# A two-layer decoder trunk on one core: where p's second layer is split, in which order the attention's end is written, and who copies the keys

## The chip, the core and the metric

The kernel runs on one core of one Trainium2 chip. A core has TensorE (PE in the profile, with PEld for its weight loads), VectorE (DVE), ScalarE (ACT), GpSimd (POOL) and SyncE (SP), each with an instruction queue of its own that runs in order, and DMA engines that move data between HBM and SBUF, the 128-partition working memory. TensorE writes its sums to PSUM, from which VectorE and ScalarE read them. The metric is the device time of one execution in microseconds; the kernel before took 1311.96 us (median of three runs, 1311.76 to 1312.21).

## The reference, cut to what matters

Batch 1, 512 tokens, 1024 features, two layers. Layer 0 mixes tokens with a causal convolution module, layer 1 with differential attention of 8 heads, each with two query/key parts of 64 features and values of 128. After each mixer stand a SwiGLU feed-forward network (hidden size 2816) and a gated embedding `p` (two layers of 512 x 256).

```python
def diff_attention(x, w_qkv, q_g, k_g, ..., sub_g, w_o, rel_bias, lambda_init):
    q, k, v = jnp.split(x @ w_qkv, 3, axis=-1)
    q = rms_norm(q.reshape(B, S, N_HEADS, 2, HEAD_DIM), q_g) * (HEAD_DIM ** -0.5)
    k = rms_norm(k.reshape(B, S, N_HEADS, 2, HEAD_DIM), k_g)
    ...
        logits = jnp.einsum('bhcqd,bhckd->bhcqk', q_blk, k) + bias[None, :, None]
        probs = jax.nn.softmax(jnp.where(dist >= 0, logits, -jnp.inf), axis=-1)
        w = probs[:, :, 0] - lam * probs[:, :, 1]
        return jnp.einsum('bhqk,bhkd->bhqd', w, v)
    ...
    o = rms_norm(o, sub_g) * (1.0 - lambda_init)
    return o.reshape(B, S, N_HEADS * V_DIM) @ w_o

for i in range(DEPTH):
    u = rms_norm(h, mixer_norm_g)
    h = h + mixer(u)                                   # conv (i = 0) or attention (i = 1)
    h = h + swiglu(rms_norm(h, ffn_norm_g[i]), w_gate, w_up, w_down)
    gate = sigmoid(rms_norm(h, ple_norm_g[i]) @ ple_w_gate[i])
    h = h + gate * (p[i] @ ple_w_proj[i])
```

All tensors are float32. The kernel keeps that accuracy with float32r matmuls by splitting each operand into a high part (a cast) and a low part (the rest): one product is three matmuls.

## The kernel before

**Split operands.** `weight()` loads 512 KB into one of two raw buffers (`wraw`, SP's queue, L146), casts it on ScalarE into one of four high buffers (`whi`, L149) and subtracts on VectorE, or on GpSimd where it is told to, into one of four low buffers (`wlo`, L150). `mm3()` (L155 to L157) is the three matmuls of one product. Weights are read in the order in which `_layout()` packs them, so the order of the calls of `weight()` is the order of the loads. `pfeatures()` (L249 to L255) loads the two halves of p through the same raw buffers (L252), casts (L253) and subtracts (L254) into the buffers that it is given.

**Buffers.** Every tile has a tag with a number of buffers, and a new tile of that tag waits until an old one has been read for the last time. PSUM has eight banks: four `mm` (sums), two `sc` (scores), two `tp` (transposes). In the attention, tags A0 to A15 hold the split input u and, from the end of the projections on, the split head outputs `ot`; B0 to B7 hold the split values (B0 to B3: heads 0 to 3, a tile for each block of 128 tokens; B4 to B7: heads 4 to 7); C0 to C5 hold two pairs of heads' split queries and keys, two buffers each; D0 to D5 hold unscaled head outputs, one each, head 6 after head 0 and head 7 after head 1.

**Projections.** `QKV` (L80) lists six slabs: queries and keys of the four pairs of heads ("q", 0 to 3) and values of two groups of four heads ("v", 0 and 1), in the order q0, v0, q1, q2, v1, q3. A slab has four weights and four blocks of 128 tokens, each block 24 matmuls of 512 columns (`tokens()`). For a query block, `unit()` scales and squares it on ScalarE, sums per head on VectorE, takes the power on GpSimd (L214), multiplies on GpSimd (L721); `unit_end()`, called inside the next block, transposes it on TensorE (L727) and splits it. A key of 64 features is stored in the half of the partitions that belongs to its part c ("own"); the score product needs its high part in the other half too, since the low part of the query lies there. In the kernel before that copy is a GpSimd instruction (L740), after ScalarE's cast of the own half (L736).

**Attention.** 32 steps, one for each head and block of queries. Each has three stages: `stage_s` (scores L772 and L773, minimum and shift on VectorE L775, exponential on ScalarE L779, the combination of the two softmaxes L782 to L784), `stage_t` two steps later (transposes L792, split L794 and L795) and `stage_a` three steps later (sum over values L808 and L809; after a head's last block the head's norm, L820 to L830). `stage_o` (L834) transposes a finished head and splits it. The stages stand in one list; 63 of its 96 are called between the projections' matmuls (`take`), as many as the paces in `QKV` say.

**The attention's end.** After the projections (L871 to L908) the rest of the list is called by `step()`, one stage a call, which also calls `stage_o` for heads that are due. `pfeatures(1, ...)` comes first, into C0 and C1; then eight times `project()` (the product of p with its weight, two `mm3`, copied out by ScalarE at L271), with a step before and two within; then `linear()`, the output product: the first two chunks of 128 features together, with a step after each `mm3`, the other six one by one, each with a weight of its own. Each chunk is added to h (L905), and the norm of the next layer begins on it.

**Who orders the work.** The program is written with a tile framework that puts each engine's instructions into a fixed order before the run, from a modelled timeline: written order gives the rank, and where the model sees an instruction not ready, a later one of the same engine may go ahead of it. At run time each engine follows that order and waits at semaphores.

Of the kernel before, what the change touches and what calls it, by code (L numbers as in the profile page):

```python
# [69 lines left out]
        TAPS += [(_c, j) for j in range(0, PE_TAPS[_c], 4)]  # L70


KDUP = "G"
HALVES = slice(0, DH), slice(DH, P)
LT = 2
LA = 3
# [8 lines left out]
def trunk(ctx, tc, xT, pT, wts, diag, dww, vec, rel, onehot, lamv, out):  # L85
# [9 lines left out]
    def sb(shape, tag, bufs, dt=F32):  # L95
        uid[0] += 1
        return pool.tile(shape, dt, tag=tag, name=f"{tag}_{uid[0]}", bufs=bufs)
# [40 lines left out]
    def weight(n=1024, pieces=1, between=(), eng=V):  # L138
        i = wnext[0]
        wnext[0] += 1  # L140
        raw = sb([P, 1024], "wraw", 2)
        hi = sb([P, 1024], "whi", 4, F32R)
        lo = sb([P, 1024], "wlo", 4, F32R)
        for k in range(pieces):
            cut = slice(k * n // pieces, (k + 1) * n // pieces)
            loaded[0] = nc.sync.dma_start(raw[:, cut], wts[i, :, cut])  # L146
            if k < len(between):
                between[k]()
            A.copy(hi[:, cut], raw[:, cut])  # L149
            eng.tensor_tensor(lo[:, cut], raw[:, cut], f(hi[:, cut]), ALU.subtract)  # L150
        return hi, lo
# [7 lines left out]
    def wpart(w, k):  # L159
        return tuple(t[:, k * P : (k + 1) * P] for t in w)  # L160

    def both(t):
        return t[:, 0], t[:, 1]
# [85 lines left out]
    def pfeatures(layer, parts):  # L249
        for k, (hi, lo) in enumerate(parts):  # L250
            raw = sb([P, 1024], "wraw", 2)[:, :S]
            nc.sync.dma_start(raw, pT[layer, :, k * S : (k + 1) * S])  # L252
            A.copy(hi, raw)  # L253
            (G if layer == 0 else V).tensor_tensor(lo, raw, f(hi), ALU.subtract)  # L254
        return parts  # L255
# [3 lines left out]
    def project(ph, m, w, o, step=lambda: None):  # L259

        acc = mm()
        for k in range(2):
            mm3(
                acc,
                wpart(w, 2 * (m % 4) + k),
                ph[k],
                k == 0,
                k == 1,
            )
            step()  # L270
        A.copy(o, acc)  # L271
        return o
# [261 lines left out]
            if c >= 2:  # L534
                V.tensor_tensor(z[c - 2][1], y[c - 2], f(z[c - 2][0]), ALU.subtract)

    def linear(n_in, src, consume, group0=1, before=None, after=None, first=0):


        m = 0  # L540
        while m < NC:
            g = group0 if m == 0 else 1
            ws = [weight(n_in * P, eng=G if m == 0 and i >= g - first else V) for i in range(g)]
            accs = [mm() for _ in range(g)]
            for k in range(n_in):
                if before:
                    before(k)
                for w_, a_ in zip(ws, accs):
                    mm3(a_, wpart(w_, k), src[k], k == 0, k == n_in - 1)
                    if after:  # L550
                        after()
            for i in range(g):
                consume(m + i, accs[i])
            m += g
# [112 lines left out]
    def slab(n=0):  # L667
        ws = [weight(eng=G if i < n else V) for i in range(4)]
        return [
            tuple(t[:, j * S : (j + 1) * S] for t in ws[k])  # L670
            for k in range(4)
            for j in range(2)
        ]
# [50 lines left out]
    def unit_end(pair, tb, q):  # L724
        t = tp()
        for i in range(4):
            T.transpose(t[:, i * P : (i + 1) * P], q[:, i * P : (i + 1) * P], ident)  # L727
        t4 = t.rearrange("p (h c t) -> p h c t", h=2, c=2)
        cut = slice(tb * P, (tb + 1) * P)
        qs, ks, kl = qk[pair][0:2], qk[pair][2:4], qk[pair][4:6]  # L730

        qg, kg = gains[:, 0:1], col("k_g")
        for c in range(2):
            own, other = HALVES[c], HALVES[1 - c]
            A.activation(qs[c][own, :, cut], t4[own, :, 0], AF.Copy, scale=qg[own])
            A.activation(ks[c][own, :, cut], t4[own, :, 1], AF.Copy, scale=kg[own])  # L736
            if KDUP == "A":
                A.activation(ks[c][other, :, cut], t4[own, :, 1], AF.Copy, scale=kg[own])
            else:
                G.tensor_copy(ks[c][other, :, cut], f(ks[c][own, :, cut]))  # L740
        for c in range(2):
            own, other = HALVES[c], HALVES[1 - c]
            V.scalar_tensor_tensor(
                qs[c][other, :, cut], t4[own, :, 0], qg[own], f(qs[c][own, :, cut]), ALU.mult, ALU.subtract)
            V.scalar_tensor_tensor(
                kl[c][own, :, cut], t4[own, :, 1], kg[own], f(ks[c][own, :, cut]), ALU.mult, ALU.subtract)
# [87 lines left out]
    def stage_o(hd):  # L834
        t = tp()
        for i in range(4):
            T.transpose(t[:, i * P : (i + 1) * P], osb[hd][:, i * P : (i + 1) * P], ident)  # L837
        hi = sb([P, S], f"A{2 * hd}", 1, F32R)
        lo = sb([P, S], f"A{2 * hd + 1}", 1, F32R)
        split_scaled(t, gains[:, 1:2], hi, lo)  # L840
        ot[hd] = (hi, lo)
# [4 lines left out]
    for n in range(len(todo) + LA):  # L846
        for stage, at in ((stage_s, n), (stage_t, n - LT), (stage_a, n - LA)):
            if 0 <= at < len(todo):
                stages.append((n, partial(stage, *todo[at])))

    def take(n):
        got, stages[:n] = [s for _, s in stages[:n]], []
        return got

    waiting = None
    for what, at, pace in QKV:
        ws = slab(GLO if at > 0 else 0)
        for tb in range(4):
            between = take(3 * pace[tb])
            between += [None] * (6 - len(between))  # L860
            if waiting:
                between.append(partial(unit_end, *waiting))
                waiting = None
            if what == "v":
                values(at, ws, tb, between)
            else:
                waiting = unit(at, ws, tb, between)
    unit_end(*waiting)


    done = [0]  # L871

    def step():
        if stages:
            n, s = stages.pop(0)
            s()
        else:
            n = 99
        while done[0] < NH and (n - LA - 3) // 4 > done[0]:
            stage_o(done[0])  # L880
            done[0] += 1

    ph = pfeatures(1, [both(sb([P, 2, S], t, 2, F32R)) for t in ("C0", "C1")])
    pp = []
    for m in range(NC):
        if m % 4 == 0:
            w = weight()
        step()
        if m < 2:
            o = sb([P, S], f"D{m + 2}", 1)  # L890
        elif m % 2 == 0:
            o2 = sb([P, 2, S], f"C{m // 2 + 1}", 2)
            o = o2[:, 0]
        else:
            o = o2[:, 1]
        pp.append(project(ph, m, w, o, step))

    def heads_until(k):
        while done[0] <= k:
            step()  # L900

    norm = Norm("ffn_g1")

    def add_attn(m, acc):
        V.tensor_tensor(h[m], acc, h[m], ALU.add)  # L905
        norm.chunk(m)

    linear(NC, ot, add_attn, 2, heads_until, step)  # L908
    n2 = Norm("ple_g1")
    ffn(norm, n2)  # L910

# [131 lines left out]
```

## Time and profile before

| What | us |
|---|---|
| median of three runs | 1311.96 |
| the profiled execution, its own time | 1313.88 |
| its span | 1312.1 |
| TensorE busy in the span | 1276.4 |
| VectorE | 759.3 |
| ScalarE | 526.9 |
| GpSimd | 276.1 |
| the first query block is scaled (L711) | 650.0 |
| the last projection's last matmul starts | 806.63 |
| first product of p's second layer starts | 819.75 |

A row of the stages' view gives a stretch of the span, its length, each engine's busy time in it with the number of instructions, TensorE's granted clock as a share of full speed, the mean busy share of the DMA engines and GB/s. A row of the waits gives who waited for whom: microseconds in total, number of waits, the longest. A row of the timeline gives start, duration, engine, line, operation, output and input tile, how many instructions are merged into it and, in brackets, how long the engine sat idle before it and what released it. Matmuls are pipelined: one may start before the last one's end, so the distance of their starts, not their duration, is what each costs. A row of the groups gives count, busy time, mean of one in nanoseconds, and idle time before them.

### The profile page before, as it was taken

What the parts mean: (1) busy time and instruction counts of PE and PEld (TensorE: products, weight loads), DVE (VectorE), ACT (ScalarE), POOL (GpSimd) and SP (SyncE); (2) the same over time, 40 slices, a digit from 0 to 9 for tenths busy, and PEclk for the clock granted to TensorE, in tenths of its full rate; (3) what the DMA queues carried; (4) which work ended last, traced back from release to release, by engine and by line L of the source; (5) the groups of instructions that cost most, each with busy time, mean ns of one, the idle gap of its engine ahead of it and who ended that gap; (6) DMA issues with size and microseconds to landing.
All of it is one profiled execution on the core that took longest, in us unless ns stands there. A gap on an engine that the chain in (4) does not pass through costs nothing. (4 is left out here: it accounts for less than half of the span.)

```text
span 1312.1 us, 15285 instructions
## 1 busy us (share of the span) xinstructions
PE 1276.4 (97%) x5830; PEld 1047.4 (80%) x5830; DVE 759.3 (58%) x1168; ACT 526.9 (40%) x832; POOL 276.1 (21%) x219
## 2 busy tenths in 40 slices
PE   8999889999999999999999998999999999999998
PEld 5787668888888888888888886778888888888887
DVE  6998866544344434455678888945543344334445
ACT  5644255332123212253566767734332233223332
POOL 4839533000000000022345534122000000000030
PEclk8999889999999999999999998999999999999999
DMA  5554203332333232232222221213233323222231
GB/s 193 182 179 156 81 32 113 96 97 80 113 96 96 81 112 96 77 116 94 72 97 81 86 75 49 97 33 128 97 96 97 96 97 97 96 96 88 80 122 64
DMA packets 44534, 129.21 MB, mean 98 GB/s; under 512 B 5123, under 2 KB 8835, under 8 KB 44460
## 3 DMA queue, kind: packets, MB, share of 16 engines
q1 hardware_dynamic: 42912, 125.84, 29.2%
q10 hardware_dynamic: 1548, 2.39, 0.6%
q8 instruction: 46, 0.75, 0.2%
q14 instruction: 28, 0.23, 0.1%
HBM read 124.52 MB, written 3.69 MB: 98 GB/s over the span
## 5 line engine op out<-in xcount | busy, mean ns | idle before, releaser
L149 ACT CAST whi<-wraw 128x1024 fp32r<-128x1024 f32 (+2 forms) x214 | 218.5, 1026 | 563.5 <-PE mm L157 363.1
L155 PE MATMUL mm<-A,wlo 128*128 128x512 f32 (+1 forms) x1096 | 425.6, 392 | 9.5 <-ACT A L533 5.9
L156 PE MATMUL mm<-A,whi 128*128 128x512 f32 (+1 forms) x1096 | 428.9, 392 | 0.7 <-DVE A L170 0.5
L157 PE MATMUL mm<-A,whi 128*128 128x512 f32 (+1 forms) x1096 | 426.5, 390 | 0.0
L150 DVE TENSOR_TENSOR wlo<-wraw,whi 128x1024 fp32r<-128x1024 f32 (+2 forms) x207 | 257.5, 1248 | 66.6 <-ACT whi L149 66.2
L155 PEld LDWEIGHTS mm<-A,wlo 128*128 128x128 f32 x1096 | 207.2, 189 | 55.2 <-ACT A L533 6.7
L156 PEld LDWEIGHTS mm<-A,whi 128*128 128x128 f32 x1096 | 207.0, 189 | 48.0 <-DVE A L170 3.8
L157 PEld LDWEIGHTS mm<-A,whi 128*128 128x128 f32 x1096 | 207.0, 189 | 43.3 <-issue 1.3
L189 POOL TENSOR_TENSOR acc<-acc,wk 128x512 f32<-128x512 f32 x42 | 68.6, 1634 | 786.7 <-issue 673.3
L156 PE MATMUL mm<-B,whi 128*128 128x512 f32 x352 | 137.5, 391 | 0.0
L157 PE MATMUL mm<-B,whi 128*128 128x512 f32 x352 | 137.5, 391 | 0.0
L155 PE MATMUL mm<-B,wlo 128*128 128x512 f32 x352 | 137.1, 391 | 0.0
L591 DVE TENSOR_TENSOR h<-mm,h 128x512 f32<-128x512 f32 x48 | 33.0, 691 | 123.1 <-PE mm L157 123.0
L583 DVE TENSOR_TENSOR big<-mm,rb 128x512 f32<-128x512 f32 x44 | 30.4, 691 | 126.2 <-PE mm L157 126.2
L581 DVE TENSOR_TENSOR big<-mm,rb 128x512 f32<-128x512 f32 x44 | 30.4, 691 | 99.0 <-PE mm L157 92.6
L157 PEld LDWEIGHTS mm<-B,whi 128*128 128x128 f32 x352 | 66.1, 188 | 14.5
L156 PEld LDWEIGHTS mm<-B,whi 128*128 128x128 f32 x352 | 66.0, 188 | 14.3
L155 PEld LDWEIGHTS mm<-B,wlo 128*128 128x128 f32 x352 | 66.1, 188 | 14.2
L157 PE MATMUL mm<-whi,A 128*128 128x512 f32 x192 | 75.6, 395 | 0.0
L156 PE MATMUL mm<-wlo,A 128*128 128x512 f32 x192 | 75.0, 396 | 0.0
L155 PE MATMUL mm<-whi,A 128*128 128x512 f32 x192 | 74.8, 396 | 0.0
L214 POOL TENSOR_TENSOR r<-v,mhalf 128x8 f32<-128x8 f32 (+1 forms) x31 | 47.4, 1530 | 114.6 <-DVE v L212 92.4
(207 smaller groups left out, 1439.0 us busy)
## 6 DMA issues: line engine op xcount, KB each, us to landing
wraw<-in_wts SPq DMA_DIRECT2D x194, 512.0 KB, 3.5
wraw<-in_wts SPq DMA_DIRECT2D x16, 384.0 KB, 2.9
D<-in_diag SPq DMA_DIRECT2D x19, 256.0 KB, 4.7
C<-in_diag SPq DMA_DIRECT2D x12, 256.0 KB, 5.5
h<-in_xT SPq DMA_DIRECT2D x8, 256.0 KB, 5.3
bias<-scr ACTq DMA_DIRECT2D x8, 256.0 KB, 3.5
out_t<-h SPq DMA_DIRECT2D x7, 256.0 KB, 2.0
wraw<-in_wts SPq DMA_DIRECT2D x4, 256.0 KB, 4.8
```

Source lines behind the costliest of these rows:

```text
L149: A.copy(hi[:, cut], raw[:, cut])
L150: eng.tensor_tensor(lo[:, cut], raw[:, cut], f(hi[:, cut]), ALU.subtract)
L155: T.matmul(acc, al, bh, start=first, stop=False)
L156: T.matmul(acc, ah, bl, start=False, stop=False)
L157: return T.matmul(acc, ah, bh, start=False, stop=last)
L189: self.eng.tensor_tensor(self.acc, self.acc, sq, ALU.add)
L214: last_pow[0] = G.tensor_tensor(r[:, :n], v[:, :n], mhalf[:, :n], ALU.pow)
L581: V.tensor_tensor(tg, pg, rb, ALU.mult)
L583: V.tensor_tensor(tu, pu, rb, ALU.mult)
L591: V.tensor_tensor(h[m], acc, h[m], ALU.add)
```

## The change

Three things are changed.

1. The second layer's p is split during the last query slab: `pfeatures(1, ...)` is called after that slab's four weights, before its first block of tokens, into tiles of tags B0 and B1 (the values of heads 0 to 3, token blocks 0 and 1). Before it was called after the projections, into C0 and C1.
2. The end is written as a loop over the remaining steps. First p's two weights and the output product's first two are requested. Each turn of the loop calls all stages of one step, then `stage_o` for heads that are due, then one piece of `fill`: two `factor()` (one chunk of p's product), five `first_sums(k)` (head k's part of the first two output chunks, six matmuls), two `factor()`. After the loop come the last head's `stage_o`, the other four `factor()` and `first_sums` of 5 to 7. `linear()` goes on with the third chunk; its hooks for steps are gone.
3. The keys' copy to the other half of the partitions is a transfer issued on ScalarE's queue, in place of a GpSimd instruction: 32 of them, 64 KB each (64 partitions, two rows of 512 bytes).

```diff
-KDUP = "G"
...
-    def linear(n_in, src, consume, group0=1, before=None, after=None, first=0):
+    def linear(n_in, src, consume, group0=1, first=0, start=0):
-        m = 0
+        m = start
         while m < NC:
...
             for k in range(n_in):
-                if before:
-                    before(k)
                 for w_, a_ in zip(ws, accs):
                     mm3(a_, wpart(w_, k), src[k], k == 0, k == n_in - 1)
-                    if after:
-                        after()
...
             A.activation(ks[c][own, :, cut], t4[own, :, 1], AF.Copy, scale=kg[own])
-            if KDUP == "A":
-                A.activation(ks[c][other, :, cut], t4[own, :, 1], AF.Copy, scale=kg[own])
-            else:
-                G.tensor_copy(ks[c][other, :, cut], f(ks[c][own, :, cut]))
+            nc.scalar.dma_start(f(ks[c][other, :, cut]), f(ks[c][own, :, cut]))
...
+    def take_to(n):
+        got = [s for at, s in stages if at < n]
+        del stages[: len(got)]
+        return got
...
         ws = slab(GLO if at > 0 else 0)
+        if at == 3:
+            ph = pfeatures(1, [both(sb([P, 2, S], f"B{k}", 1, F32R)) for k in range(2)])
         for tb in range(4):
...
-    done = [0]
-    def step():
-        if stages:
-            n, s = stages.pop(0)
-            s()
-        else:
-            n = 99
-        while done[0] < NH and (n - LA - 3) // 4 > done[0]:
-            stage_o(done[0])
-            done[0] += 1
-    ph = pfeatures(1, [both(sb([P, 2, S], t, 2, F32R)) for t in ("C0", "C1")])
+    pw = [weight(), weight()]
+    wo = [weight(), weight()]
     pp = []
-    for m in range(NC):
-        if m % 4 == 0:
-            w = weight()
-        step()
+    oaccs = []
+    def factor():
+        m = len(pp)
         if m < 2:
             o = sb([P, S], f"D{m + 2}", 1)
         elif m % 2 == 0:
-            o2 = sb([P, 2, S], f"C{m // 2 + 1}", 2)
-            o = o2[:, 0]
+            o2[0] = sb([P, 2, S], f"C{m // 2 + 1}", 2)
+            o = o2[0][:, 0]
         else:
-            o = o2[:, 1]
-        pp.append(project(ph, m, w, o, step))
-    def heads_until(k):
-        while done[0] <= k:
-            step()
+            o = o2[0][:, 1]
+        pp.append(project(ph, m, pw[m // 4], o))
+    o2 = [None]
+    def first_sums(k):
+        if k == 0:
+            oaccs.extend([mm(), mm()])
+        for w_, a_ in zip(wo, oaccs):
+            mm3(a_, wpart(w_, k), ot[k], k == 0, k == NC - 1)
+    fill = [factor] * 2 + [partial(first_sums, k) for k in range(5)] + [factor] * 2
+    done = 0
+    while stages:
+        n = stages[0][0]
+        for s in take_to(n + 1):
+            s()
+        while done < NH and (n + 1 - LA - 3) // 4 > done:
+            stage_o(done)
+            done += 1
+        if fill and (not hasattr(fill[0], "args") or fill[0].args[0] < done):
+            fill.pop(0)()
+    stage_o(NH - 1)
+    for _ in range(NC - len(pp)):
+        factor()
+    for k in range(5, NH):
+        first_sums(k)
...
-    linear(NC, ot, add_attn, 2, heads_until, step)
+    for m in range(2):
+        add_attn(m, oaccs[m])
+    linear(NC, ot, add_attn, start=2)
```

## The prediction

> **What bounds the kernel now.** I read the head of the page and the forty slices first, then the busy times by stage, the waits of TensorE around the one place where it is not full, and the timeline of that place.
>
> ```profile
> span 1312.1 us, 15285 instructions
> PE 1276.4 (97%) x5830; PEld 1047.4 (80%) x5830; DVE 759.3 (58%) x1168; ACT 526.9 (40%) x832; POOL 276.1 (21%) x219
> PE   8999889999999999999999998999999999999998
> PEclk8999889999999999999999998999999999999999
> ```
>
> TensorE is the bound: 97% busy, and between the start and the last slice its only dip is at slice 25 (32.8 us each, so 787 to 820), where the clock row dips too. That is the attention's end, so the stages there come next.
>
> ```profile
> core 0: us, PE busy (x) PEld busy (x) DVE busy (x) ACT busy (x) POOL busy (x), PEclk, DMA share, GB/s
> 660.00:805.00 145.00, 142.73 (x748) 121.22 (x747) 116.72 (x307) 96.28 (x222) 68.85 (x67) 1.00 0.22 74
> 805.00:820.00 15.00, 8.77 (x45) 7.19 (x44) 14.63 (x37) 12.27 (x29) 5.36 (x7) 0.76 0.27 87
> 820.00:835.00 15.00, 13.06 (x64) 10.15 (x64) 14.11 (x38) 11.99 (x27) 3.95 (x4) 0.89 0.43 141
> 835.00:852.00 17.00, 17.00 (x107) 15.15 (x106) 14.77 (x48) 13.46 (x36) 2.05 (x2) 1.00 0.19 63
> 852.00:872.00 20.00, 19.79 (x105) 16.72 (x104) 7.07 (x20) 4.04 (x8) 4.09 (x4) 1.00 0.01 2
> 872.00:880.00 8.00, 5.47 (x26) 4.03 (x24) 5.84 (x7) 4.89 (x7) 1.88 (x2) 1.00 0.10 31
> ...
> 810.00:815.00 5.00, 2.20 (x10) 1.50 (x10) 4.92 (x14) 4.42 (x13) 2.79 (x3) 0.79 0.35 75
> 815.00:820.00 5.00, 2.59 (x11) 2.52 (x12) 4.91 (x14) 3.10 (x6) 1.27 (x2) 0.50 0.47 187
> 820.00:825.00 5.00, 5.00 (x18) 4.08 (x18) 4.86 (x13) 3.17 (x7) 2.54 (x4) 0.68 0.66 213
> ```
>
> From 660 to 805 TensorE lacks 2.27 of 145 us. From 805 to 880 it lacks 6.23 + 1.94 + 0 + 0.21 + 2.53 = 10.91 us. On top it ran below full clock: 2.20 x (1 - 0.79) + 2.59 x (1 - 0.50) + 5.00 x (1 - 0.68) = 0.46 + 1.30 + 1.60 = 3.36 us of busy time were the clock's. So **14.3 us** are there to win in this stage, of which 9.6 lie in 805 to 825 (idle 15 + 5 - 8.77 - 5.00 = 6.23, and all the 3.36). VectorE is 14.63 of 15 busy there, then 14.11 of 15, then 14.77 of 17: it is the second bound until about 852.
>
> ```profile
> PE sc L772 <- DVE st L775: 4.2, 4, 1.7
> PE sc L772 <- DVE st L783: 2.5, 1, 2.5
> PE mm L155 <- DVE wlo L150: 1.8, 1, 1.8
> PE tp L727 <- DVE C L745: 1.0, 1, 1.0
> PE mm L155 <- ACT A L169: 0.8, 1, 0.8
> PE sc L772 <- POOL C L740: 0.2, 1, 0.2
> ```
>
> TensorE waits for the softmax's VectorE work because it has nothing else queued. Why not, the timeline tells:
>
> ```profile
> 781.33 2.32 SPq L252 DMA_DIRECT2D wraw<-in_pT  x2
> ...
> 794.61 1.04 POOL L830 TENSOR_TENSOR D<-D,r 128x512 f32<-128x512 f32 x1 [0.34 <-ACT acc L779]
> ...
> 806.63 0.40 PE L157 MATMUL mm<-whi,A 128*128 128x512 f32 x1
> ...
> 809.01 1.16 ACT L253 CAST C<-wraw 128x512 fp32r<-128x512 f32 x2
> 812.18 0.68 DVE L254 TENSOR_TENSOR C<-wraw,C 128x512 fp32r<-128x512 f32 x1
> 813.06 0.68 DVE L254 TENSOR_TENSOR C<-wraw,C 128x512 fp32r<-128x512 f32 x1
> 812.89 8.05 SPq L146 DMA_DIRECT2D wraw<-in_wts  x4
> 816.88 1.04 ACT L149 CAST whi<-wraw 128x1024 fp32r<-128x1024 f32 x1 [2.06 <-DMA wraw<-in_wts]
> 818.10 1.22 DVE L150 TENSOR_TENSOR wlo<-wraw,whi 128x1024 fp32r<-128x1024 f32 x1
> 819.75 0.78 PE L155 MATMUL mm<-C,wlo 128*128 128x512 f32 x1
> ...
> 877.99 0.50 PE L155 MATMUL mm<-A,wlo 128*128 128x512 f32 x1 [1.75 <-DVE wlo L150]
> ```
>
> p's two raw parts are issued at 781.33 into the only two raw weight buffers and sit there until they are split at 809.01 to 813.7, because their split form goes to C0 and C1, which the queries and keys of heads 4 and 5 hold. Only at 812.89, as the first part is done (812.18 + 0.68), can the next weight be issued; it is cast at 816.88, its low part made at 818.10, and the first p product runs at 819.75, though the last queries' matmul ended at about 806.9. From 806.9 to 819.75 TensorE has only scores, transposes and sums that wait on each other.
>
> **The change part by part.** The unit first: matmuls of 512 columns one after another.
>
> ```profile
> 878.80 0.40 PE L155 MATMUL mm<-A,wlo 128*128 128x512 f32 x1
> ...
> 893.12 0.39 PE L155 MATMUL mm<-A,wlo 128*128 128x512 f32 x1
> ```
>
> 63 matmuls start from the first to the second, so one takes 14.32 / 63 = 0.227 us. A `factor()` and a `first_sums()` are 6 each, 1.36 us; the eight factors hold 10.9 us.
>
> *p's parts in B0 and B1.* These hold values of heads 0 to 3, free when head 3's sums are out; head 3 is the fourth of eight to be scaled, at 794.61, and its sums end some microseconds before. Two casts (1.16 us on ScalarE) and two subtractions (2 x 0.68 on VectorE) move from 809 to 813.7 to some 790 to 796, inside a stretch where VectorE is 116.72 of 145 and ScalarE 96.28 of 145 busy and TensorE full: costed at nothing, cover the queries' matmuls; without it, 1.16 + 0.68 = 1.8 us. The two raw buffers come free 17 us earlier, so SP's queue moves on: p's two weights can land long before 806 and wait only for the four split buffers of the last queries, which free one by one in the last block of tokens. Best case they are ready at 806.9, when the factors can start; worst, VectorE (4.92 and 4.91 of 5 in two of the slices) pushes the two subtractions behind stage work, some 2 x 1.25 = 2.5 us each way, and the factors start near 812. With 10.9 us of factors against a pocket of 12.9 (806.9 to 819.75) the pocket can be nearly filled. What stays: the waits in which each engine's fixed order misses by a fraction, and the outputs of factors 0 and 1, which need D2 and D3, hence heads 2 and 3 transposed. The bounds are 9.6 (all) and 9.6 x 5 / 12.9 = 3.7 less, 5.9; if ready only after 815 about 3. I take **-7.0**.
>
> The granted clock is part of this: 0.50 in 815 to 820, and 0.68 while TensorE was 5.00 of 5.00 busy, so it returned only after some 3 us of steady work. The Trainium skill (TensorE: Matmul & The Clock Gate, Part 1: The HAM clock gate) has two states, half and full, and a full busy window of about 3.4 us before the full one returns; the trace agrees with its means. By that rule the clock's share is all or nothing: 9.0 or 5.6 for the sum of 8.0 below.
>
> *Written order of the end.* Before, three stages and a factor alternate, then one stage per three output matmuls; after, all stages of one step and then one of two factors, five first sums, two factors, and the last four factors and three first sums behind the last head. VectorE's work until the last scores (852) stays the same but for 1.36 moved away, so this stretch gets no shorter than VectorE allows: 14.11 + 14.77 of 32 us from 820. I cost the 1.94 us idle in 820 to 835 as kept: factors spent earlier are missing there, the first sums stand in. At the end, 0.8 us go to the last head's transposed output and 1.8 to a weight's low part at 877.99 (four buffers held by the four open output chunks). After, four factors and two first sums (36 x 0.227 = 8.2 us) cover the first, and the third and fourth chunk's weights take the buffers that p's weights leave, so the next ones aren't all due at once. Of 2.53 I take **-2.0**; bounds 0 (the stall moves to a later chunk) and -2.5.
>
> *Keys by transfers.* 32 GpSimd copies go; 32 issues on ScalarE's queue come.
>
> ```profile
> L740 POOL CAST C<-C 64x256 fp32r<-64x256 f32 x32 | 14.6, 455 | 21.1 <-ACT C L736 19.9
> L647 ACTq DMA_DIRECT2D bias<-scr x8: 326/326/455, 647.6 to 812.0; - x8
> C<-pi SPq DMA_DIRECT2D x12, 64.0 KB, 3.3
> B<-po SPq DMA_DIRECT2D x12, 64.0 KB, 1.9
> ```
>
> TensorE waited 0.2 us for these copies near the end (above); GpSimd is not the bound, so its 14.6 us are worth nothing but that. A transfer of the same 64 KB landed 1.9 to 3.3 us after issue against 0.46, so the copied half comes 1.5 to 2.8 us later. Its reader is the score stage of that token block, one or more blocks later (24 matmuls, 5.4 us, each); only in the last two blocks is the lag near the cover. Each issue takes 0.33 us, and it must wait for the cast just ahead of it on the same engine; behind it queue the second half's casts, the exponentials and the splits of transposed weights. 32 x 0.33 = 10.4 us on an engine with 48.7 of 145 us free. No ScalarE-issued copy of ScalarE's own result is in the trace, so bounds: -0.2 (the wait above gone) and +10.4 (every issue shown on TensorE). It lies nearer the low end, as nearly all falls where TensorE is full and fed from four accumulators, but eight issues (2.6 us) fall in 804 to 821 where ScalarE is 12.27 of 15: **+1.0**.
>
> Sum: -7.0 - 2.0 + 1.0 = -8.0. The profiled execution took 1313.9 us with a span of 1312.1; the median of the three shown is 1311.96, so the span goes to 1304.1 and the median to about **1304.0**.
>
> **The rivals.** *Everything is filled*: also the waits of 820 to 835 go, and the copies cost nothing: -14.3 plus some 1.3 of unavoidable misses, 1299. For it: there is work enough (10.9 of factors, 6.8 of first sums). Against: VectorE's 43.5 busy us (14.63 + 14.11 + 14.77) must pass before the last head can end.
>
> *VectorE is the bound*: the low parts come at 812 or later and idle time only moves behind 820, where factors are now missing: -3 from the first pocket, 1309. For it: 4.92 and 4.91 of 5; against: VectorE is 14 of 15 there because stages ran ahead while nothing else could.
>
> *ScalarE's queue turns the sign*: each transfer holds ScalarE's queue until the cast before it is written, then 0.33 us; the transposes' buffers come free later, q and k of the next block with them, and score stages slip. With every issue shown: -9 + 10.4, and two more waits of the mean length of those on L775 (4.2 / 4 = 1.05 each), = +3.5, 1315.5. It decides from an exposure of 9 / 32 = 0.28 us for each copy, less than one issue. For it: ScalarE at 82% from 805 to 820; against: 34% free before. The Trainium skill (DMA: Bandwidth & Descriptors, Anatomy of one DMA) says that a wait of a DMA is taken on the issuing sequencer before dispatch, which is this mechanism; no row of before shows such a wait.
>
> *The change doesn't do what it says*: each engine's order is planned from a model, and p's splits may still be planned late, or the raw buffers be held by another load: 1312.
>
> **How the numbers follow.** Forecast 0.46 (about 1301.5 to 1307), all filled 0.14, VectorE 0.17, ScalarE's queue 0.16, not as said 0.07. Range 1298.5 to 1314: the first four reach into it, the upper part of the fourth is left out. I count 0.2% (2.6 us) as what can be told from no change: faster is the first three less a little (0.75), same 0.07, slower 0.18.
>
> **What would show it.** Right: L254 near 790, weights of p cast by 806, the first p product within 2 us of the last queries' matmul, clock 1.00 from 805 to 825, TensorE idle under 4 us from 805 to 880. Wrong: idle of TensorE before L772 between 660 and 805 well over 2.3 us, with ScalarE's casts (L735, L736) spread out around the transfers; or idle on VectorE's results in 820 to 850 that was not there. If the copies' exposure on TensorE is above 0.28 us each, the forecast's sign is wrong.

## The result, and the profile after

| | before | after |
|---|---|---|
| median, us (six runs each, same chip) | 1312.11 (1311.76 to 1313.13) | 1317.47 (1313.67 to 1318.71) |
| ratio, 95% interval | | 1.0037 [1.0024, 1.0050] |

The changed kernel is slower; the forecast was 8 us faster. Executions of one kernel spread here by several microseconds: the profiled one of the changed kernel took 1313.67 (span 1311.9), the other five 1317.2 to 1318.7, so a second profile of it was taken (after_again below, 1317.79, span 1316.0).

Two rows of the forty slices of the changed kernel:

```profile
PE   8999989999999999999999998999999999999998
PEclk8999989999999999999999999899999999999999
```

TensorE's dip in slice 25 is still there, and the clock's, now in slice 26. The busy times by stage, in the columns of before:

```profile
660.00:805.00 145.00, 140.89 (x739) 118.94 (x738) 121.45 (x306) 97.02 (x224) 51.59 (x38) 1.00 0.28 90
805.00:820.00 15.00, 9.44 (x50) 7.54 (x49) 14.69 (x37) 11.95 (x29) 6.71 (x5) 0.88 0.56 175
820.00:835.00 15.00, 14.65 (x72) 12.53 (x73) 11.82 (x35) 8.71 (x21) 2.26 (x2) 0.78 0.04 10
835.00:852.00 17.00, 14.23 (x87) 11.58 (x86) 15.45 (x54) 11.99 (x34) 3.78 (x4) 1.00 0.02 4
852.00:872.00 20.00, 19.82 (x105) 16.72 (x105) 6.50 (x13) 7.27 (x13) 2.79 (x3) 1.00 0.14 50
872.00:880.00 8.00, 6.25 (x28) 4.83 (x27) 5.32 (x6) 4.20 (x6) 2.11 (x2) 1.00 0.14 42
```

From 805 to 880 TensorE lacks 5.56 + 0.35 + 2.77 + 0.18 + 1.75 = 10.61 us, where it lacked 10.91. The clock takes 9.44 x 0.12 + 14.65 x 0.22 = 4.4 us of 805 to 835, where by the same two rows of before it took 8.77 x 0.24 + 13.06 x 0.11 = 3.5. And from 660 to 805 it now lacks 4.11 us in place of 2.27.

A kernel's time is cut most cleanly at three starts on TensorE: the first projection matmul of layer 1, the last one, and the last of the feed-forward network's first 384 matmuls, which follow the output product. (One expectation below calls this last cut the last output matmul. The output product itself ends 88.9 us earlier, at 899.70 before and 899.46 after, and these 88.9 us are the same to 0.03 us in all profiles but keys_glo0's, where they are 89.1. So the end's differences are made ahead of the feed-forward network.) Before (first and last of these; the middle one, 806.63, stands in the prediction), then the change's second profile:

```profile
633.37 0.39 PE L155 MATMUL mm<-whi,A 128*128 128x512 f32 x1
988.56 0.39 PE L157 MATMUL mm<-A,whi 128*128 128x512 f32 x1
```

```profile
632.56 0.39 PE L154 MATMUL mm<-whi,A 128*128 128x512 f32 x1
810.86 0.39 PE L156 MATMUL mm<-whi,A 128*128 128x512 f32 x1
992.46 0.39 PE L156 MATMUL mm<-A,whi 128*128 128x512 f32 x1
```

The *projections* took 806.63 - 633.37 = 173.26 us before and 810.86 - 632.56 = 178.30 after; the *end* 988.56 - 806.63 = 181.93 before and 992.46 - 810.86 = 181.60 after. In the change's first profile they are 175.49 and 182.08. What follows the last cut is 323.5 us in all three. So **the end, from which 9.0 us were expected, gave nothing, and the projections, where 1.0 was to be lost, lost 2.2 to 5.0.** All experiments below are read by these two numbers, taken from each profile in the same way. They leave out the start of layer 1, which wanders by 3 us from one execution to the next (630.4 to 633.5), but not the granted clock: the two profiles of the change differ by 2.8 us in the projections. Each is from one profile only, so the ratio of the whole times stands beside them.

**The projections.** Timelines of GpSimd, VectorE and TensorE in the second profile, and then the busy times by stage, with the clock in the third column from the end:

```profile
742.22 1.04 POOL L822 TENSOR_TENSOR D<-D,r 128x512 f32<-128x512 f32 x1 [1.86 <-DVE st L774]
743.22 2.37 POOL L149 TENSOR_TENSOR wlo<-wraw,whi 128x1024 fp32r<-128x1024 f32 x1
742.21 1.07 DVE L775 SCALAR_TENSOR_TENSOR st<-st,lam 128x1 f32<-128x1 f32 x1
743.31 2.82 DVE L776 SCALAR_TENSOR_TENSOR big<-rb,st,big 128x512 f32<-128x512 f32 x1
746.52 0.33 PE L764 MATMUL sc<-C,C 128*128 128x128 f32 x1 [2.02 <-DVE st L767]
748.08 1.09 PE L722 MATMUL tp<-ident,big 128*128 128x128 f32 x4 [0.72 <-DVE wtl L787]
```

```profile
740.00:745.00 5.00, 4.50 (x25) 3.59 (x23) 4.89 (x9) 4.21 (x7) 3.14 (x3) 1.00 0.23 66
745.00:750.00 5.00, 2.76 (x12) 2.41 (x13) 4.97 (x13) 3.26 (x9) 1.63 (x2) 0.74 0.23 59
750.00:755.00 5.00, 5.00 (x15) 3.89 (x14) 4.55 (x11) 3.62 (x8) 4.28 (x4) 0.58 0.49 180
```

On GpSimd a head's scaling (L822) and a weight's low part (L149) stand back to back, 742.22 to 745.59. Beside them two VectorE steps of the softmax are held: L775 takes 1.07 and L776 2.82 us, each ending right after the GpSimd instruction beside it. Scores on TensorE wait 2.02 us for what comes behind, a transpose 0.72 more. Then the clock reads 0.74 and 0.58. In the first profile the same two waits are there, to the hundredth, but the clock stays at 1.00. In the second it takes 2.76 x 0.26 + 5.00 x 0.42 = 2.8 us in these rows: that is the difference between the two profiles. In before the same low part lies elsewhere:

```profile
740.16 2.39 POOL L150 TENSOR_TENSOR wlo<-wraw,whi 128x1024 fp32r<-128x1024 f32 x1
740.39 2.19 DVE L212 TENSOR_SCALAR v<-v 128x4 f32<-128x4 f32 x1 [0.46 <-POOL r L214]
```

```profile
740.00:745.00 5.00, 5.00 (x28) 4.20 (x27) 4.61 (x5) 2.82 (x6) 5.00 (x4) 1.00 0.25 70
```

It holds up a VectorE instruction too, but a small one that TensorE isn't waiting for (5.00 of 5 busy). The low part stands eight microseconds ahead of the next head's scaling there. What changed is GpSimd's planned order: low part, then scaling before; scaling, then low part after. The Trainium skill (SBUF — State Buffer, SBUF: two separate sides) says that VectorE, with two inputs from SBUF, and a GpSimd instruction that reads SBUF contend for a port pair that one of them holds for its whole instruction while the other stands still. The trace agrees: L776 was through 0.54 us after the end of the GpSimd instruction, and takes 0.75 alone (below).

**The end.** ScalarE's and VectorE's rows for p and its weights, and TensorE's around the products, in the change's first profile:

```profile
787.00 0.69 DVE L253 TENSOR_TENSOR B<-wraw,B 128x512 fp32r<-128x512 f32 x1
788.53 0.68 DVE L253 TENSOR_TENSOR B<-wraw,B 128x512 fp32r<-128x512 f32 x1
805.72 1.04 ACT L148 CAST whi<-wraw 128x1024 fp32r<-128x1024 f32 x1
806.25 0.39 PE L156 MATMUL mm<-whi,A 128*128 128x512 f32 x1
808.43 0.39 PE L154 MATMUL mm<-B,wlo 128*128 128x512 f32 x1
811.07 0.39 PE L156 MATMUL mm<-B,whi 128*128 128x512 f32 x1
819.80 0.66 PE L764 MATMUL sc<-C,C 128*128 128x384 f32 x1 [2.08 <-DVE v L211]
820.58 1.05 PE L829 MATMUL tp<-ident,D 128*128 128x128 f32 x4
826.67 0.57 ACT L270 COPY D<-mm 128x512 f32<-128x512 f32 x1
```

p is split at 787 to 789 and the first product starts at 808.43, 1.8 us behind the end of the queries' last matmul (806.25 + 0.39), as forecast. But only factors 0 and 1 follow, 12 of 48 matmuls, the last at 811.07; ScalarE can copy them out only from 826.67. The list of `fill` goes on with the first sums, which need transposed heads, and the first heads are transposed at 820.58. From 812 to 820 TensorE waits again for the softmax: of 805 to 820 it is idle 5.56 us, where before it was 6.23.

### The profile page after: what moved, and what is told of

Same layout as the page of the kernel before. It is cut to its first block, busy times and chain, and to the rows that moved or that the text cites. A ratio compares the mean times of both kernels' runs of the same rounds, so it can differ in the third digit from the quotient of the medians.

```text
span 1311.9 us, 15291 instructions
## 1 busy us (share of the span) xinstructions
PE 1275.6 (97%) x5830; PEld 1045.4 (80%) x5830; DVE 762.6 (58%) x1168; ACT 527.7 (40%) x832; POOL 262.4 (20%) x187
## 4 chain that ended last, share of the span: by engine, by line
PE 82%; DVE 9%; POOL 3%; issue 2%; ACT 1%; DMA 1%; SPq 0%; ACTq 0%; DVEq 0%; POOLq 0%
PE mm L154 26%; PE mm L155 26%; PE mm L156 26%; DVE sc L401 3%; POOL wk L390 2%; DVE wlo L149 2%; PE mm L800 1%; DVE B L401 1%; PE sc L764 1%; PE sc L765 1%; PE tp L784 0%; PE tp L722 0%; ACT C L389 0%; POOL B L435 0%; DVE big L470 0%
## 5 line engine op out<-in xcount | busy, mean ns | idle before, releaser
L149 DVE TENSOR_TENSOR wlo<-wraw,whi 128x1024 fp32r<-128x1024 f32 (+2 forms) x207 | 258.7, 1253 | 69.3 <-ACT whi L148 69.1
L154 PE MATMUL mm<-B,wlo 128*128 128x512 f32 x368 | 143.6, 392 | 0.3 <-ACT C L270 0.3
L155 PE MATMUL mm<-B,whi 128*128 128x512 f32 x368 | 143.7, 391 | 0.0
L156 PE MATMUL mm<-B,whi 128*128 128x512 f32 x368 | 143.7, 390 | 0.0
L154 PEld LDWEIGHTS mm<-B,wlo 128*128 128x128 f32 x368 | 69.1, 188 | 15.3 <-ACT C L270 0.5
L156 PEld LDWEIGHTS mm<-B,whi 128*128 128x128 f32 x368 | 69.1, 188 | 15.2
L155 PEld LDWEIGHTS mm<-B,whi 128*128 128x128 f32 x368 | 69.1, 188 | 14.8
```

Of the source, the lines that this page charges most:

```text
L154: T.matmul(acc, al, bh, start=first, stop=False)
L155: T.matmul(acc, ah, bl, start=False, stop=False)
L156: return T.matmul(acc, ah, bh, start=False, stop=last)
```

## The experiments

Projections and end are from one profile of each, in us; the ratio is to the kernel before, run on the same chip, with its 95% interval. Before: 173.26, 181.93, from one profile. The experiments ran on four chips, on which the median of before was 1312.76 (first four rows), 1314.92 (p_order to p8_D), 1314.45 (keys_glo0 to first8_D) and 1313.21 (the last four). So whole times in microseconds compare only within such a group; across groups the ratio does, and a difference of some 2 us between a stretch and before's says little without it.

| kernel | projections | end | ratio |
|---|---|---|---|
| after_again | 178.30 | 181.60 | 1.0032 [1.0021, 1.0044] |
| keys_only | 178.34 | 183.36 | 1.0051 [1.0039, 1.0063] |
| p_only | 173.31 | 184.53 | 1.0008 [0.9999, 1.0016] |
| order_only | 173.26 | 184.77 | 1.0024 [1.0014, 1.0033] |
| p_order | 173.30 | 185.08 | 1.0014 [1.0005, 1.0023] |
| p_free | 173.25 | 181.07 | 0.9980 [0.9971, 0.9989] |
| p8 | 173.33 | 183.87 | 1.0007 [0.9995, 1.0018] |
| p8_D | 173.33 | 179.51 | 0.9970 [0.9959, 0.9982] |
| keys_glo0 | 171.57 | 185.31 | 0.9995 [0.9985, 1.0006] |
| keys_act | 172.66 | 189.21 | 1.0028 [1.0018, 1.0037] |
| keys_both | 178.09 | 185.73 | 1.0044 [1.0030, 1.0057] |
| first8_D | 173.29 | 178.38 | 0.9959 [0.9945, 0.9973] |
| after_glo0 | 171.59 | 181.21 | 0.9979 [0.9970, 0.9989] |
| after_first8 | 178.36 | 177.22 | 0.9996 [0.9987, 1.0005] |
| after_first8_glo0 | 171.58 | 176.64 | 0.9942 [0.9929, 0.9954] |
| before_glo0 | 170.76 | 186.10 | 0.9992 [0.9981, 1.0004] |

### The change's parts alone

*The change again*, for its second profile:

> The changed kernel once more, for a second profile: five of its six times lay near 1317.5 and the profiled one at 1313.7. Both theories: 1316 to 1318. Theory A (the fill runs dry because its outputs and sums have no room, and the idle time that follows drops the clock for a varying time): the profile shows TensorE's idle of 805 to 880 still near 10.6 us, and the extra microseconds of the long executions as more time below full clock. Theory B (ScalarE's queue is held by the key transfers): the extra time shows as TensorE idle before score matmuls between 650 and 805.

*Keys by transfers alone:*

```diff
-                G.tensor_copy(ks[c][other, :, cut], f(ks[c][own, :, cut]))
+            nc.scalar.dma_start(f(ks[c][other, :, cut]), f(ks[c][own, :, cut]))
```

> Before, with only the keys copied by transfers. Theory A: within 1.5 us of before (1310.6 to 1313.6). Theory B: slower by 4 to 6 us (1316 to 1318), with TensorE waiting for scores or transposes of queries between 650 and 805.

*p's split early alone* (into B0 and B1, within before's end):

```diff
+        if at == 3:
+            ph = pfeatures(1, [both(sb([P, 2, S], f"B{k}", 1, F32R)) for k in range(2)])
...
-    ph = pfeatures(1, [both(sb([P, 2, S], t, 2, F32R)) for t in ("C0", "C1")])
```

> Before, with only p split in the values' buffers during the last queries. Theory A: the first two products of p run at once after the last queries' matmuls and then stall for the buffers of heads 2 and 3, so only some 2.7 us of the pocket of 9.6 are filled: 1309 to 1312. If early weights alone filled the pocket as forecast: 1304 to 1306. Theory B: as Theory A, since the keys are not touched.

*The written end alone* (p split late, in C0 and C1, behind the projections):

> Before, with only the end in its written order; p still goes through C0 and C1. Theory A: the pocket of 805 to 825 stays as before and the fill's fixed order adds idle time behind it: slower by 2 to 5 us (1314 to 1317). Theory B: within 1.5 us of before.

Of these kernels, those with the transfers lose in the projections, 178.3 (175.49 in the change's first profile), and those without them don't, 173.3. The parts don't add up: each alone makes the end longer (by 1.4, 2.6 and 2.8 us), the three together don't. keys_only (1319.84) and p_only (1314.12) came out slower than any theory on record gave. In p_only 18 factor matmuls ran before 820, but the clock read 0.51 from 820 to 835, where before's was 0.89.

*Parts 1 and 2 without the transfers:*

> Changed kernel with the keys' copy given back to GpSimd (parts 1 and 2 of the change without part 3). Theory 'keys cost it' (the re-timed GpSimd queue puts a VectorE/GpSimd clash on TensorE's path at 740 to 750): TensorE idles under 1 us from 740 to 780 as in before (0.66), the time is 1312 to 1315, 2.5 to 5 us under the whole change. Rival 'the end costs it': the idle of 805 to 855 decides, the time stays at 1316 to 1318.

The projections are back at 173.30, but the end is 185.08, the longest of the first five: both the keys and the end cost, and neither theory alone has it. Its time, 1315.79, lies between the two theories' ranges, but it was taken where before's median was 1314.92, and the theories were reckoned from the group with 1312.76; by its ratio it is 1314.6 there, within the first theory's range. Against the change, which differs in the keys alone, its end is 3.0 to 3.5 us longer: behind the projections the transfers seem to help there, and why stays open.

### Why the pocket stays empty

*p_only with the first two factors' outputs in a free buffer:*

```diff
-            o = sb([P, S], f"D{m + 2}", 1)
+            if m == 0:
+                o2 = sb([P, 2, S], "C0", 2)
+            o = o2[:, m]
```

> p split early as in p_only (1314.12), and the outputs of factors 0 and 1 go to a free buffer of tag C0 in place of D2 and D3. Theory 'the fill stops at D2 and D3': both sums are copied out by 815 in place of 828 to 830, more factors follow at once, TensorE's idle in 805 to 835 falls from 8.1 us to under 4, the time is 1308 to 1311. Rival 'rotation of the mm banks': a factor and a head's sum over values are called in turn, so the fourth factor's bank comes behind a sum that has to wait for the softmax; then the copies come early but still only three factors run before 818, and the time stays within 1312.5 to 1315.5.

The copies come early, and still only three factors, 18 matmuls, run before 820, as many as in p_only. So D2 and D3 don't set how much is filled. That fits the rival's mechanism: in before's end a factor and a head's sum over values take a bank each in turn, and the sum waits for the softmax. No run changes the banks, so this reason is argued, not shown. The whole is nevertheless faster than p_only (0.9980 against 1.0008, end 181.07 against 184.53), as fast as the first theory gave. From 820 to 835, in steps of 5 us, the clock reads 0.50, 0.81 and 1.00, where p_only's reads 0.50, 0.50 and 0.52.

*The eight factors ahead of all remaining stages*, with the outputs in C0, and then (p8_D) in D2 and D3:

```diff
     for m in range(NC):
...
-        step()
...
-        pp.append(project(ph, m, w, o, step))
+        pp.append(project(ph, m, w, o))
```

> p split early, before's end, but all eight factors are called ahead of the remaining stages (no stage between them), with the outputs of 0 and 1 in C0. All 48 factor matmuls are then planned ahead of the last query block's transposes. Theory 'the pocket is what costs': TensorE idles under 3 us in 805 to 825 (7.5 in p_only), granted clock 0.95 or more there, time 1304 to 1308. Rival 'VectorE is the bound of the whole end': VectorE has 43.5 us of work in 805 to 852 before (14.63 + 14.11 + 14.77), which the filling doesn't shorten; the pocket is filled, but TensorE idles as much later, in 825 to 860, where the factors are missing, and the time is 1311 to 1315.

> As p8, but the outputs of factors 0 and 1 go to D2 and D3 again, so that this pair differs in the buffers alone. Theory 'the fill stops at D2 and D3': four mm banks are full after four factors, of which two can't be emptied until heads 2 and 3 are transposed; TensorE idles 3 to 6 us more than p8 in 805 to 825. Whether that is worth time follows from p8: 2 to 5 us slower than p8 if the pocket is the cost, within 1.5 us of p8 if VectorE is the bound.

Busy times of p8, then of p8_D (columns as above):

```profile
805.00:820.00 15.00, 15.00 (x77) 12.62 (x76) 14.61 (x32) 14.33 (x30) 5.17 (x7) 1.00 0.51 152
820.00:835.00 15.00, 11.25 (x51) 8.67 (x51) 11.27 (x30) 8.53 (x22) 3.71 (x4) 0.77 0.21 70
835.00:855.00 20.00, 16.04 (x100) 13.44 (x100) 17.55 (x63) 13.37 (x38) 3.26 (x3) 0.95 0.01 2
```

```profile
805.00:820.00 15.00, 13.51 (x68) 11.11 (x67) 14.67 (x33) 12.89 (x28) 5.10 (x6) 1.00 0.42 123
820.00:835.00 15.00, 13.94 (x82) 11.36 (x80) 12.60 (x38) 12.02 (x27) 2.83 (x4) 1.00 0.24 70
835.00:855.00 20.00, 17.04 (x97) 14.34 (x95) 16.31 (x57) 11.70 (x35) 4.40 (x4) 0.83 0.01 2
```

p8 fills the pocket to the brim, 15.00 of 15 at full clock, and gains nothing: 3.75 + 3.96 us are idle behind it, and the clock falls there. The last of the 48 matmuls starts at 820.07, just as the last query block's transposes (820.47) begin a second run of short waits. In p8_D factors 0 and 1 are copied out only at 826.39 and 828.91, so the last ones are pushed behind 820 (the last starts at 822.11): the idle time from 805 to 855 is 1.49 + 1.06 + 2.96 = 5.51 in place of 7.71, and it is faster by 0.4%. My expectation for this pair had the sign wrong. I read it so: what counts is not that the filling work runs early but that some is left for each hole. The pair differs in two buffers alone, but it is one pair.

*The same cure in the written order*, p_order with one edit:

```diff
-    fill = [factor] * 2 + [partial(first_sums, k) for k in range(5)] + [factor] * 2
+    for _ in range(8):
+        factor()
+    fill = [partial(first_sums, k) for k in range(5)]
```

> Parts 1 and 2 of the change (keys by GpSimd, as p_order) with a single edit of the written order: all eight factors are listed ahead of the loop, and the loop's filling work is the five first sums alone. From the last projection matmul to the last output matmul p_order took 185.1 us, p8_D 179.5, before 181.9. Theory 'the written list starves the pocket' (two factors stand in it before the first sums, which need heads that are transposed only at 820): 179 to 181 us here, the whole time 1309 to 1311, and TensorE idle in 805 to 885 at 8 to 9 us in place of 12.2. Rival 'the loop itself costs' (all stages of one step at a time): 183 to 185 us, 1313 to 1316.

p_order, then first8_D:

```profile
805.00:820.00 15.00, 9.88 (x49) 7.35 (x47) 14.63 (x35) 11.46 (x26) 3.78 (x6) 0.86 0.49 153
820.00:835.00 15.00, 12.67 (x52) 9.94 (x53) 10.05 (x30) 8.02 (x19) 4.17 (x6) 0.68 0.01 1
835.00:855.00 20.00, 17.21 (x108) 14.34 (x108) 18.15 (x62) 14.22 (x39) 3.76 (x4) 1.00 0.02 3
```

```profile
805.00:820.00 15.00, 13.45 (x70) 11.07 (x69) 14.67 (x36) 12.63 (x27) 5.49 (x7) 1.00 0.44 129
820.00:835.00 15.00, 13.91 (x83) 11.42 (x82) 12.63 (x36) 12.30 (x30) 2.43 (x4) 1.00 0.19 65
835.00:855.00 20.00, 16.85 (x101) 14.22 (x100) 16.43 (x57) 11.91 (x34) 4.40 (x4) 0.91 0.01 1
```

Idle time from 805 to 855 falls from 5.12 + 2.33 + 2.79 = 10.24 to 1.55 + 1.09 + 3.15 = 5.79 us, and the clock in the first two stretches goes from 0.86 and 0.68 to 1.00. (Counted over 48 us from each kernel's own last projection matmul, 806.27 and 803.92, it is 10.16 and 5.61.) The end is 6.7 us shorter. The order of the list was the cost, not the loop. The same edit is made twice more below, with the transfers.

### What the keys cost

*Transfers, and no low parts on GpSimd* in the projections (`GLO` tells how many weights of a slab have theirs made there):

```diff
-GLO = 1
+GLO = 0
```

> Before with keys by transfers (keys_only), and the four weights' low parts that GpSimd makes for the projections' slabs made by VectorE instead. From the first projection matmul to the last one is 173.3 us in before and 178.3 in keys_only; of those 5.0, 2.1 are TensorE's idle time at 740 to 750 and 2.9 a granted clock below 1.00 behind it. Theory 'clash': the 2.4 us GpSimd subtraction at 744 holds up VectorE's combination of the two softmaxes (2.8 us in place of 0.75). Without it the stretch takes 173.3 to 174.5 us, with no VectorE instruction of that line over 1.2 us. Rival 'landing': the keys' copies come 2 us late and the scores behind them: the stretch stays at 175.5 or more.

The same softmax step in that kernel, with nothing of GpSimd beside it:

```profile
740.30 0.75 DVE L781 SCALAR_TENSOR_TENSOR big<-rb,st,big 128x512 f32<-128x512 f32 x1
```

L781 (L776 in the change) takes 0.75 us, never more in the projections, and these take 171.57, less than before's. The transfers are all still there, so neither their issue nor their landing is what costs 5 us.

*Copies on ScalarE* (before's own switch, `KDUP = "A"`, a third cast), *and transfers with GpSimd kept busy* (this edit beside the transfer):

```diff
+            junk = sb([P, P], "junk", 1)
+            G.tensor_copy(junk[own], f(ks[c][own, 0, cut]))
```

> Before with the keys' copy made by ScalarE itself (a third cast from PSUM): no GpSimd copy and no transfer, but some 0.47 us more of ScalarE for each of 32. Theory 'clash': GpSimd's subtraction is planned ahead of the head norm's product again, as in before, so the stretch from the first to the last projection matmul takes 173.2 to 174.5 us. Rival 'ScalarE's time': what the change costs is time on ScalarE's queue (0.6 us an issue); then this kernel loses about as much as keys_only in the same stretch, 176 to 179 us.

> Keys by transfers, and beside each a GpSimd copy of half the size into a scratch tile that nobody reads, so that GpSimd's queue is about as full as in before. If the cost in the projections comes from GpSimd's work falling at another time, the stretch from the first to the last projection matmul is 173.2 to 175 us; if it comes from the transfers' issue or landing, 177 to 179 us.

With ScalarE's copies the low part is planned ahead of the head's scaling again, as in before:

```profile
739.85 2.39 POOL L150 TENSOR_TENSOR wlo<-wraw,whi 128x1024 fp32r<-128x1024 f32 x1
742.34 1.04 POOL L830 TENSOR_TENSOR D<-D,r 128x512 f32<-128x512 f32 x1
```

and the projections take 172.66. With the transfers and half-size copies into scratch the order is still the other one, and they take 178.09:

```profile
740.15 1.04 POOL L829 TENSOR_TENSOR D<-D,r 128x512 f32<-128x512 f32 x1 [1.27 <-DVE st L781]
741.15 2.36 POOL L150 TENSOR_TENSOR wlo<-wraw,whi 128x1024 fp32r<-128x1024 f32 x1
```

keys_act has no copies on GpSimd and keeps before's order; keys_both has some and loses it. So the number of GpSimd's instructions doesn't decide the order. In all five profiles with the transfers and `GLO = 1` it is scaling, low part; in all nine with `GLO = 1` and no transfers it is low part, scaling. Why the planner's model orders so with the transfers in the program stays open, and no run changes the order alone. The end of keys_act is the longest of all in its profile, 189.21, though its whole time is only 0.28% above before's.

### Both causes in the whole change

The change with `GLO = 0`; with the edit of the list; with both; and before with `GLO = 0`:

> The whole change with one edit: the low parts of the projections' weights that GpSimd makes are made by VectorE. Theory 'clash': the projections take 171.5 to 173.5 us from their first to their last matmul, in place of the 175.5 and 178.3 of the change's two profiles; the end is as in the change (181.6 to 182.1) or up to 2 us worse, since the keys kernel with the same edit had 185.3; the whole is 1310 to 1314. Rival 'the transfers themselves': 175 us or more, 1316 to 1319.

> The whole change with one edit: all eight factors listed ahead of the loop, the five first sums alone as filling work in it. Theory: the end falls from 181.6 to 182.1 us to 177 to 180 as in first8_D (178.4), while the projections keep their 175.5 to 178.3; the whole 1312 to 1315. Rival 'the transfers' landing decides the end': the last query block's keys land 2 to 5 us after issue, all the scores behind them slip, and the end stays over 181 us, the whole over 1315.5.

> The whole change with both edits. If both causes are what the change lost, their effects add: projections 171.5 to 173.5 us, end 177 to 181, the whole 1305 to 1309, faster than before (1312) by more than 0.2%. If the low parts on VectorE push the last weights' back in the end, the end is 181 to 185 and the whole 1310 to 1313.

> Before with the low parts on VectorE alone: the control for the two others. If GpSimd's subtraction does no harm where before has it, the projections take 172.5 to 173.5 us and the time is 1311 to 1315; if it does some harm there too, the 1.6 us wait before L775 at 710 goes, 171.5 us, 1310 to 1312.

Each edit mends its own part and leaves the other: 171.59 and 181.21, then 178.36 and 177.22. Together, 171.58 and 176.64: **1305.64 us (1303.75 to 1306.58), 0.9942 [0.9929, 0.9954] of before**, the fastest kernel of the study. That it lies near the change's forecast is luck: 5.3 us are from the end, where 9.0 were forecast, and 1.7 from the low parts, which the forecast didn't touch.

In before, the first of the two edits is worth nothing: the projections fall by 2.5 us to 170.76, so GpSimd's low parts cost something there too, but the end takes 186.10. It starts earlier, and the first product of p still comes 13.0 us behind the last projection matmul (814.96 - 801.95; before 13.1). What the transfers cost by themselves in the projections is 171.57 - 170.76 = 0.8 us; with GpSimd's low parts it is 178.34 - 173.26 = 5.1.

## Why the prediction was wrong

- *The place was right*: 14.3 us are lost around 805 to 880, and after_first8_glo0 has 5.3 of them (181.93 - 176.64). *p's early split* went as worked out: subtractions at 787 and 788.5 ("near 790"), a weight cast by 806, the first product within 2 us, no cost in the projections (173.31 in p_only).
- **The step that failed first: "With 10.9 us of factors against a pocket of 12.9 (806.9 to 819.75) the pocket can be nearly filled."** The sum of the work was compared with the length of the pocket, and not with what is ready in it. Of eight factors the written list puts two ahead of the first sums, and those need heads that come at 820: 12 matmuls, 2.7 us by the row unit of 0.227. That list stood in the diff. The clause on the outputs of factors 0 and 1 named a real wait, but neither runs p8 and p8_D nor first8_D, which keeps D2 and D3, make it the limit. Expected -7.0; in place of it TensorE's idle time in 805 to 820 fell from 6.23 to 5.56 us, 2.77 us of new idle time came in 835 to 852 (half of it, 1.45 at 849.98, a first sum that waits for ScalarE's split of a head), and the end moved by +0.15 and -0.33. With the list mended it moved by -3.6 to -5.3 (first8_D, after_first8, after_first8_glo0): the term was too large as well, since 7.4 us of 805 to 885 stay idle in the best kernel.
- *And it would not have sufficed*: p8 filled that pocket completely and stayed at 183.87. The rival "VectorE is the bound" had the result (idle time moves behind 820, where factors are missing), though not through a late low part.
- *The end's -2.0*: heads do finish sooner, but that is worth nothing by itself:

```profile
864.88 0.22 PE L809 MATMUL mm<-B,wtl 128*128 128x128 f32 x1
```

```profile
857.53 0.22 PE L801 MATMUL mm<-B,wtl 128*128 128x128 f32 x1
```

  The last sum over values starts 58.25 us behind the last projection matmul before, and 51.28 after. But 123.68 us follow until the last cut before, and 130.80 after: three factors (18 matmuls, 859.03 to 862.88) and 18 more matmuls of the output product than before are still to come, 4.1 us each. The wait of 1.8 us on a weight's low part that I had counted as gone is in the changed kernel's waits as well, so that of the 2.53 us idle in 872 to 880 only 0.78 went:

```profile
PE mm L154 <- DVE wlo L149: 1.8, 1, 1.8
```

- **The second failing step: "GpSimd is not the bound, so its 14.6 us are worth nothing but that."** True of the busy time, but the term of +1.0 put a change of the planned order at nothing. With the transfers in the program a low part lies behind a head's scaling, beside VectorE's softmax, and the projections lose 2.2 to 5.0 us; without low parts on GpSimd they lose 0.8. That the 0.8 is near +1.0 is in part luck: an issue took 0.60 us in place of 0.33, and in the end, where eight issues fall on a busy ScalarE, the transfers made nothing longer in the changed order (177.22 in after_first8 against 178.38 in first8_D). The rival "ScalarE's queue turns the sign" came nearest to the time (1315.5) by another mechanism: keys_glo0 has all 32 transfers, and keys_act 32 more casts of 0.47 us on ScalarE, and against before neither loses in the projections (171.57 and 172.66).
- *The clock*: 3.5 us lost in 805 to 835 before and 4.4 after, as the holes were moved and not closed.

## What to carry to other kernels

Filling work is worth what is ready at each hole: check the list it stands in and what is left for the next hole before comparing its sum with the idle sum. Finishing a chain sooner gains nothing on a saturated engine if the filling work is thereby put behind the chain. Giving a small job to another engine can move other instructions in the planned order: look beside what the long GpSimd instructions will come to lie.

## What the runs showed of the hardware

- The same two waits of TensorE (2.02 and 0.72 us) left the clock at 1.00 in one profile of the changed kernel and took it to 0.58 in the other; the projections took 175.49 and 178.30 us. With the same clash keys_only, keys_both and after_first8 had 178.34, 178.09 and 178.36.
- A transfer from SBUF to SBUF on ScalarE's queue, 64 KB over 64 partitions, held the queue for 0.60 us, against 0.33 for the bias loads there, and landed 2.1 us after issue at the median:

```profile
C<-C ACTq DMA_DIRECT2D x32, 64.0 KB, 2.1
```

```profile
816.35 0.33 ACTq L647 DMA_DIRECT2D bias<-scr  x1
816.71 0.60 ACTq L737 DMA_DIRECT2D C<-C  x1
823.19 0.66 PE L769 MATMUL sc<-C,C 128*128 128x384 f32 x1 [5.92 <-DMA C<-C]
```

  The second fence is of keys_only, where the longest landing took 7.0 us: TensorE waited 5.92 us for one. In the change's first profile no wait of TensorE on one shows.
